# A hybrid diffusion block on one core: another order of steps where the MLP begins

## The chip, the cores and the metric

The kernel runs on one core of one Trainium2 chip. The metric is the device time of one execution in microseconds (us): the median over the runs shown, lower is better. A core has engines that run side by side, each with its own queue of instructions worked off strictly in order: TensorE (PE, with its weight loads as PEld), VectorE (DVE), ScalarE (ACT), GpSimd (POOL) and SyncE (SP). Transfers (DMA) are issued by SP, ACT and POOL; only those of POOL can add to what is already at their destination.

## What is computed

One layer of a diffusion backbone over 1024 tokens of width 1024, with 256 context tokens. What matters here is the seam between its two halves: the output projection of the mixer, the residual with its two row norms, and the first matrix of the MLP.

```python
attn_x = _neighbourhood_attention(q_x, k_x, v_x, k_c, v_c, rpb[l])
mix_x = jnp.concatenate([_pool_mixer(u_x, pool_w[l], pool_scale[l]), attn_x], axis=-1) @ w_out[l]
x = x + gt1 * _rmsnorm(mix_x, g_post_mix[l])
y_x = _sq_relu_mlp(_modulate(x, g_pre_mlp[l], sh2, sc2), w_mlp_in[l], w_mlp_out[l])
x = x + gt2 * _rmsnorm(y_x, g_post_mlp[l])
```

`_modulate` is a row norm times (1 + scale) plus shift, `_sq_relu_mlp` is `square(relu(h @ w1)) @ w2` with `w1` 1024 x 4096.

## The kernel before

**Products.** Every float32 product is made of three matrix products: each operand is split into a high part (a cast on ACT) and a low part (a difference on DVE), and `three` (lines 168 to 170) issues high x high, low x high and high x low as 128x512 matmuls. The large products (output projection, both MLP matrices) use a scheme with seven products of half-size blocks instead of eight. For the first MLP matrix the tokens are cut in two halves (row tiles 0 to 3 and 4 to 7) and the 1024 channels in two halves, which gives the token blocks B11, B21 (first token half, lower and upper channels) and B12, B22 (second token half), and four combinations T1 = B12 - B11, T2 = B22 - T1, T3 = B22 - B12, T4 = B21 - T2. The weights are cut into A11, A12, A21, A22, with combinations S1 to S4 made on the fly by `weight_parts` (line 1207).

**Before the MLP.** The region `added` (line 1043) does most of the output projection for row tiles 0 to 3, then their rows: `out_less` (a difference of sums, DVE), `out_square` (its mean square, ACT), `out_gated` (times the gate, DVE), `row_root` (one over root: a small DVE step and one on POOL), `row_added` (the residual: DVE `xr`, a store on POOL's queue, and its mean square on ACT, `mp<-xr`), `row_second` (the second root) and `row_scaled` (DVE).

**The MLP's beginning.** `last_product` (line 1128) does the last product of the projection, `out_sums(v[t])` for t = 0 to 3, and between these makes channel pairs 0 to 2 of the first token half: eight transposes on PE into `px` (line 1114), a scale and shift on ACT into `nf` (line 1119), and the split into `thB..` (ACT, line 143) and `tlB..` (DVE, line 144), together `pair_made`. In the same list stand the row steps of tiles 4 to 7. `last_pair` (line 1160) makes pair 3 and ends the rows of tiles 4 to 7. ACT and DVE run `last_product` in exactly the order in which it is written (`in_order`, line 103), and so they do with `last_pair` and with the first call of `second_half`.

**The loop.** For p = 0, 2, 4, 6 the kernel does `first_sum` (line 1296) of p and p + 1: twelve matmuls of A11 with B11 into the bank `phx`, then a copy of it on ACT (`s1`, line 1304), stored to memory for p < 4. Then `second_sum` (line 1309) of both adds A12 x B21 to the same bank, for which the copy must have been taken, and squares its positive part on ACT (lines 1246, 1247). Between these `second_half` (line 1172) makes the second token half: 32 transposes, then T2, T1, T3, and after the loop B22 and T4, each as a combination on DVE (lines 1184 to 1189) and a split. PE's order is that in which the program is written, from the region `added` to the last pair; outside the `in_order` parts ACT's and DVE's orders are chosen by a planner. After the loop come sixteen `block_pair`s, each starting with `phy` = S2 x T2.

**Weights.** A generator with a lookahead of four (`lookahead`, line 1269) makes the weights' splits `wpA`, `wpS` ahead of the product that uses them. Four buffers `raw` take the loaded weights, eight `hl` their splits.

Of the kernel before, what the change touches and what calls it, by code (L numbers as in the profile page):

```python
# [1 line left out]

# [8 lines left out]
F32 = mybir.dt.float32  # L11
# [68 lines left out]
def hybrid_block(ctx, tc, x, ctx_in, w_mod, b_mod, gp1, gp2, w_in, pool_w, rpb, w_out, w1, w2, vectors,  # L80
                 mask, edge, out):
    nc = tc.nc
# [59 lines left out]
    def split(src, hi, lo):  # L142
        nc.scalar.copy(hi, src)  # L143
        nc.vector.tensor_tensor(lo, src, hi.bitcast(F32), sub)  # L144

# [835 lines left out]
    with tc.tile_pool(name="ps2", bufs=6, space=PSUM) as ps2:  # L981
# [6 lines left out]
      with ExitStack() as tmp2:  # L988
# [54 lines left out]
        with tc.issue_after(projected[ET.DVE]), tc.issue_after(projected[ET.Activation]), in_order(ET.Activation, ET.DVE) as added:  # L1043
# [47 lines left out]
            for t in (6, 7):  # L1091
                out_square(1, t, c[t])
                out_gated(1, t, c[t])
# [9 lines left out]

        tok = {}
# [3 lines left out]
        def normal_pair(b, kp, both=True):  # L1108
            f = page(f"nf{b}_{kp}")
            for o in range(2):  # L1110
                k = 2 * kp + o
                pt = bank(f"px{b}_{k}")
                for i in range(4):
                    nc.tensor.transpose(pt[:, i * P : (i + 1) * P], mp1[4 * b + i][:, k * P : (k + 1) * P], ident)
                fo = f[:, o * 512 : (o + 1) * 512]
                if b and o and both:
                    nc.vector.tensor_scalar(fo, pt, a2[:, k : k + 1], s2[:, k : k + 1], mul, add)
                else:
                    nc.scalar.activation(fo, pt, AF.Identity, bias=s2[:, k : k + 1], scale=a2[:, k : k + 1])
            return f  # L1120
# [5 lines left out]


        def last_product():
            def pair_made(kp):
                plain[0, kp] = normal_pair(0, kp)  # L1130
                token_part("B11" if kp < 2 else "B21", kp % 2, plain[0, kp])

            def first_steps(t):
                c[t] = out_less(0, t, v[t - 4], u2[t - 4])
                out_square(0, t, c[t])
                out_gated(0, t, c[t])

            def last_steps(t):
                row_second(t)
                row_scaled(t)  # L1140
# [10 lines left out]
            out_sums(v[3], "A22", wt4, 3, False)  # L1151
# [8 lines left out]
        def last_pair():  # L1160
            plain[0, 3] = normal_pair(0, 3)
            token_part("B21", 1, plain[0, 3])
            row_root(7)
            row_added(7)
            for t in (4, 5, 6, 7):
                row_second(t)
                row_scaled(t)

        held = {}


        def second_half(names):
            if not held:
                nf = dict((kp, normal_pair(1, kp, kp % 2 == 0)) for kp in (0, 2, 1, 3))
                nf = [nf[kp] for kp in range(4)]
                held["b12"], held["B22"] = nf[:2], nf[2:]
                held["T1"], held["T2"] = [[page(f"t{i}_{kp}") for kp in range(2)] for i in (1, 2)]
            b12, b22, b21 = held["b12"], held["B22"], [plain[0, 2 + kp] for kp in range(2)]
            for name in names:
                for kp in range(2):  # L1180
                    t1, t2 = held["T1"][kp], held["T2"][kp]
                    src = {"T1": t1, "T2": t2, "T3": b12[kp], "B22": b22[kp], "T4": b21[kp]}[name]
                    if name == "T2":
                        nc.vector.tensor_tensor(t1, b12[kp], plain[0, kp], sub)
                        nc.vector.tensor_tensor(t2, b22[kp], t1, sub)
                    elif name == "T3":
                        nc.vector.tensor_tensor(src, b22[kp], src, sub)
                    elif name == "T4":
                        nc.vector.tensor_tensor(src, src, t2, sub)
                    token_part(name, kp, src)  # L1190

        with tc.issue_after(added[ET.DVE]), tc.issue_after(added[ET.Activation]), in_order(ET.Activation, ET.DVE) as first_part:
            last_product()
# [13 lines left out]
        def weight_parts(p, which):  # L1207
# [13 lines left out]
            for n in which:  # L1221
                if n == "S2":
                    combined("S1", a[1, 0], a[1, 1], add)
                    combined("S2", made["S1"], a[0, 0], sub)
                elif n == "S3":
                    combined("S3", a[0, 0], a[1, 0], sub)
                elif n == "S4":
                    combined("S4", a[0, 1], made["S2"], sub)
# [3 lines left out]
                split(src, blocks(w[:, :512]), blocks(w[:, 512:]))  # L1232
                yield w
# [35 lines left out]
        def lookahead(gens, n):  # L1269
            ahead = []  # L1270
            for g in gens:
                for w in g:
                    ahead.append(w)
                    if len(ahead) > n:
                        yield ahead.pop(0)
            yield from ahead

# [12 lines left out]
        parts = lookahead([early_sequence()], 4)  # L1290

        def step(ps, name, begin):
            product(ps, next(parts), name, begin)
# [40 lines left out]
        def block_pair(p, ahead):  # L1334
# [20 lines left out]
            nc.vector.tensor_tensor(c22, v, c22, add)  # L1355
# [8 lines left out]
            nc.vector.tensor_tensor(c12, z, u2, add)  # L1364
# [80 lines left out]
        for p in range(0, EARLY, 2):  # L1445
            both = [q for q in (p, p + 1) if q < EARLY]
            xs = {}
            for q in both:
                xs[q], early[q] = first_sum(q)
                if q == 0:  # L1450
                    with tc.issue_after(first_part[ET.DVE]), tc.issue_after(first_part[ET.Activation]):
                        with in_order(ET.Activation, ET.DVE):
                            last_pair()
            if p == 2:
                with in_order(ET.Activation, ET.DVE) as made_first:
                    second_half(("T2",))
            if p == 4:
                second_half(("T1",))
            if p == 6:
                second_half(("T3",))  # L1460
            for q in both:
                second_sum(q, xs[q])
        second_half(("B22", "T4"))
        parts = lookahead([sequence()], 4)
        with tc.issue_after(made_first[ET.Activation]), tc.issue_after(made_first[ET.DVE]):
# [151 lines left out]
```

## Time and profile before

| | |
|---|---|
| median of 3 runs | 1064.68 us |
| lowest, highest | 1064.08, 1065.23 us |
| the profiled execution | 1064.99 us |
| its span in the trace | 1063.2 us |
| PE busy | 1036.0 us (97%) |
| DVE, ACT, POOL busy | 713.7 us (67%), 531.4 us (50%), 84.3 us (8%) |
| mean granted clock of PE | 0.992 |

The span runs from the first to the last instruction in the trace; 1.8 us of the profiled execution lie around it. In rows of the timeline the columns are the start in us, the duration in us, the engine, the line, the operation, output <- input by the program's names, shapes and count, and in brackets how long the engine had been idle before it and what ended that. Matmuls overlap, so the pace of PE is read from the distance between two starts. In rows of groups, busy us and the mean in ns stand behind the first bar, idle time before the group and its releasers behind the second.

### The profile page before, as it was taken

The numbers are of one execution on the slowest core, as the hardware profiler recorded it, in microseconds if no ns is written. First come the engines' busy times: TensorE is split into PE (matmuls) and PEld (weight loads), VectorE is DVE, ScalarE is ACT, GpSimd is POOL, SyncE is SP. The second block draws the span as 40 slices with busy tenths as digits, with TensorE's granted clock in tenths as the row PEclk, the third lists the DMA queues.
The fourth block names the chain that finished last, engine by engine and source line by source line (L and its number), as shares of the span: only waits on it lengthen the run. The fifth ranks groups of instructions, "written<-read, shape, count | busy, mean of one in ns | idle before, by whom it ended". The sixth has DMA issues, their size and how long they took to land.

```text
span 1063.2 us, 15505 instructions
## 1 busy us (share of the span) xinstructions
PE 1036.0 (97%) x5878; PEld 851.4 (80%) x5878; DVE 713.7 (67%) x1117; ACT 531.4 (50%) x925; POOL 84.3 (8%) x141
## 2 busy tenths in 40 slices
PE   8999999999999999599999999999999999999996
PEld 6788888877888787488888888888888888888885
DVE  5535646537997598589888766665577566557586
ACT  7462021257887556667555455554463335334441
POOL 2020000051211312100000000000000000000001
PEclk9999999999999999799999999999999999999999
DMA  9905753033337777445766435345597766546556
GB/s 344 322 21 197 278 183 125 21 73 99 71 91 190 170 191 224 138 146 164 255 218 214 152 132 195 126 147 197 204 367 247 248 238 216 192 164 206 174 191 204
DMA packets 104315, 194.87 MB, mean 183 GB/s; under 512 B 7984, under 2 KB 42544, under 8 KB 104240
## 3 DMA queue, kind: packets, MB, share of 16 engines
q1 hardware_dynamic: 81888, 150.82, 43.5%
q10 hardware_dynamic: 16848, 30.44, 7.8%
q0 software_dynamic: 5504, 12.61, 5.5%
q8 instruction: 46, 0.75, 0.3%
q14 instruction: 29, 0.24, 0.1%
HBM read 147.70 MB, written 38.81 MB: 175 GB/s over the span
## 4 chain that ended last, share of the span: by engine, by line
PE 92%; ACT 3%; DMA 2%; DVE 2%; issue 1%; SPq 0%; DVEq 0%; POOLq 0%; ACTq 0%
PE pk L404 4%; PE S L718 3%; PE pa L794 3%; PE phx L169 3%; PE pyv L168 3%; PE pyz L168 3%; PE pyx L169 3%; PE pyx L168 3%; PE phv L170 3%; PE phz L170 3%; PE phv L169 3%; PE phz L169 3%; PE pyv L170 3%; PE pyz L170 3%; PE pyv L169 3%; PE pyz L169 3%
## 5 line engine op out<-in xcount | busy, mean ns | idle before, releaser
L168 PE MATMUL phx<-thB,wpA 128*128 128x512 f32 x128 | 51.9, 406 | 11.8 <-ACT thB L143 9.4
L1246 ACT ACTIVATE c<-c 128x512 f32<-128x512 f32 x48 | 30.4, 633 | 54.9 <-DVE c L1356 23.4
L741 ACT ACTIVATE sp<-sp,nm 128x640 f32<-128x640 f32 (+1 forms) x64 | 51.3, 802 | 8.9 <-DVE nm L732 8.5
L732 DVE CUSTOM_DVE_ANT_0 sp<-S,tab 128x640 f32<-128x640 f32 (+1 forms) x56 | 42.8, 802 | 17.5 <-PE S L718 11.1
L169 PE MATMUL phx<-tlB,wpA 128*128 128x512 f32 x128 | 51.6, 403 | 0.9 <-DVE tlB L144 0.9
L139 POOL TENSOR_TENSOR ry<-vy,nhalf 128x1 f32<-128x1 f32 x8 | 4.4, 550 | 597.5 <-DVE vy L137 597.5
L170 PE MATMUL phx<-thB,wpA 128*128 128x512 f32 x128 | 51.1, 399 | 0.0
L144 DVE TENSOR_TENSOR wpS<-S,wpS 128x512 fp32r<-128x512 f32 x64 | 43.7, 686 | 10.4 <-ACT wpS L143 10.4
L143 ACT CAST wpS<-S 128x512 fp32r<-128x512 f32 x64 | 39.0, 614 | 19.0 <-PE phv L170 10.2
L168 PEld LDWEIGHTS phx<-thB,wpA 128*128 128x128 f32 x128 | 24.9, 194 | 18.4 <-ACT thB L143 10.3
L1247 ACT ACTIVATE c<-c 128x512 f32<-128x512 f32 x48 | 30.3, 632 | 13.2 <-DVE sa L1319 12.4
L169 PEld LDWEIGHTS phx<-tlB,wpA 128*128 128x128 f32 x128 | 24.8, 194 | 7.0 <-DVE tlB L144 1.9
L170 PEld LDWEIGHTS phx<-thB,wpA 128*128 128x128 f32 x128 | 24.9, 194 | 5.1
L718 PE MATMUL S<-kT,q 64*128 64x384 f32 (+1 forms) x128 | 27.9, 495 | 0.4 <-DVE nm L732 0.4
L1364 DVE TENSOR_TENSOR c<-phz,u 128x512 f32<-128x512 f32 x16 | 11.0, 690 | 25.4 <-PE phz L170 25.4
L794 PE MATMUL pa<-pt,v 128*64 128x128 f32 x352 | 25.9, 279 | 0.7 <-ACT px L774 0.2
L779 DVE COPY pt<-T 128x512 f32<-128x512 f32 x32 | 21.9, 686 | 5.4 <-PE T L760 5.4
L168 PE MATMUL phy<-thT,wpS 128*128 128x512 f32 x64 | 24.9, 389 | 0.0
L169 PE MATMUL phy<-tlT,wpS 128*128 128x512 f32 x64 | 24.9, 389 | 0.0
L170 PE MATMUL phy<-thT,wpS 128*128 128x512 f32 x64 | 24.9, 389 | 0.0
L168 PE MATMUL phz<-thT,wpS 128*128 128x512 f32 x64 | 24.9, 389 | 0.0
L169 PE MATMUL phz<-tlT,wpS 128*128 128x512 f32 x64 | 24.9, 389 | 0.0
(1004 smaller groups left out, 3336.6 us busy)
## 6 DMA issues: line engine op xcount, KB each, us to landing
b<-in_w SPq DMA_DIRECT2D x64, 512.0 KB, 4.4
hrS<-hdS SPq DMA_DIRECT2D x32, 512.0 KB, 5.3
hrA<-hdA SPq DMA_DIRECT2D x24, 512.0 KB, 5.7
wm<-in_w_mod SPq DMA_DIRECT2D x16, 512.0 KB, 9.7
wa_0w<-in_w SPq DMA_DIRECT2D x16, 512.0 KB, 4.8
wa_1w<-in_w SPq DMA_DIRECT2D x16, 512.0 KB, 4.3
hdA<-c ACTq DMA_DIRECT2D x32, 256.0 KB, 2.1
hdS<-sa ACTq DMA_DIRECT2D x32, 256.0 KB, 2.7
```

The costliest lines, as they stand in the source:

```text
L143: nc.scalar.copy(hi, src)
L144: nc.vector.tensor_tensor(lo, src, hi.bitcast(F32), sub)
L168: nc.tensor.matmul(ps, ahi, bhi, start=first, stop=False, skip_group_check=more)
L169: nc.tensor.matmul(ps, ahi, blo, start=False, stop=False, skip_group_check=more)
L170: nc.tensor.matmul(ps, alo, bhi, start=False, stop=last, skip_group_check=more)
L404: nc.tensor.matmul(pks[b][j], wk(wgt, k, low, j * P, P), r, start=(k == 0 and n == 0), stop=(k == KT - 1 and n == 2))
L718: nc.tensor.matmul(S[e][:, c0 : c0 + keys.shape[1]], q[hs, cols], keys[hs], start=True, stop=True)
L732: nc.vector.tensor_tensor_reduce(out=to, in0=s, in1=bt, scale=1.0, scalar=BIG, op0=add, op1=ALU.min, accum_out=nm)
L741: nc.scalar.activation(sp, sp, AF.Exp, bias=least[i, e], scale=-1.0, accum_out=sums[i][:, e : e + 1])
L794: nc.tensor.matmul(pa[e * HD : (e + 1) * HD, cols], v[:, f : f + HD], turns[i][:, e, c] if c < 4 else fifths[i][:, :, (e + 1) * HD : (e + ...
L1246: nc.scalar.activation(r, src, AF.Relu)
L1247: nc.scalar.activation(r, r, AF.Square)
```

## The change

Four edits in the MLP's beginning, and one in how weights are made ahead.

1. **Order in `last_product`.** The rows of tiles 4 to 7 leave it, but for `out_less`; the steps of c[6] and c[7] for the other half of the columns come in from `added`. All four channel pairs of the first token half are made here, the last two with their 16 transposes in a row, ahead of the first `first_sum`.
2. **Rows in steps.** `row_steps` is a generator whose six steps are taken one after each of the first sums and second sums (none after `first_sum(3)`).
3. **Second half in steps.** `second_steps` follows with seven: the transposes and `nf` of the second half, the combinations, and one step each for the splits of T2, T1, T3, B22 and T4.
4. **Signs and adding transfers.** B21 and B12 are made with the opposite sign (`less_a2`, `less_s2`), so that every combination becomes a sum: T1' = B11 - B12 and T2 stay on DVE, T3 = B22 - B12 and T4' = T2 - B21 are made by `add_to`, a transfer on POOL's queue that adds to its destination, four of 512 KB in all. A12, A22 and S4 change sign to match (`less_split`), and two results are subtracted where they were added. In `block_pair`s and in the loop nothing else changes.
5. **Weights one by one.** `more` makes one weight part per `step`, with five made in `last_product`. The whole stretch, from `last_product` to the last `second_sum`, stands in one `in_order` for ACT and DVE, transfers that ACT issues among them.

```diff
+    def less_split(src, hi, lo):
+        nc.scalar.activation(hi, src, AF.Copy, scale=-1.0)
+        nc.vector.scalar_tensor_tensor(lo, src, -1.0, hi.bitcast(F32), mul, sub)
...
-            for t in (6, 7):
-                out_square(1, t, c[t])
-                out_gated(1, t, c[t])
...
+        def normal_pair(b, kp, pts, both=True):
+            f = page(f"nf{b}_{kp}")
+            a, d = (less_a2, less_s2) if b == (kp < 2) else (a2, s2)
...
         def last_product():
             for t in range(2):
                 out_sums(v[t], "A22", wt4, t, False)
-            first_steps(4)
-            pair_made(0)
+            first_less(4)
+            more()
+            pts = transposed(0, 0)
+            first_less(5)
+            pair_made(0, pts)
+            more()
             out_sums(v[2], "A22", wt4, 2, False)
-            row_root(4)
-            first_steps(5)
-            row_added(4)
-            pair_made(1)
+            pts = transposed(0, 1)
+            first_less(6)
+            gate_steps(1, 6)
+            pair_made(1, pts)
+            more()
             out_sums(v[3], "A22", wt4, 3, False)
-            row_root(5)
-            first_steps(6)
-            row_added(5)
-            pair_made(2)
-            row_root(6)
-            first_steps(7)
-            row_added(6)
+            pts = transposed(0, 2)
+            first_less(7)
+            pair_made(2, pts)
+            pts = transposed(0, 3)
+            more()
+            pair_made(3, pts)
+            gate_steps(1, 7)
...
+        def row_steps():
+            gate_steps(0, 4)
+            yield
+            row_root(4)
+            gate_steps(0, 5)
+            row_root(5)
+            row_added(4)
+            gate_steps(0, 6)
+            yield
+            row_second(4)
+            row_root(6)
+            row_added(5)
+            gate_steps(0, 7)
+            yield
+            row_second(5)
+            row_root(7)
+            row_added(6)
+            row_scaled(4)
+            yield
+            row_second(6)
+            row_added(7)
+            row_scaled(5)
+            yield
+            row_second(7)
+            row_scaled(6)
+            row_scaled(7)
+            yield
+
+        def second_steps():
+            nf = dict((kp, normal_pair(1, kp, transposed(1, kp), kp % 2 == 0)) for kp in (0, 2, 1, 3))
+            b12, b22, b21 = [nf[0], nf[1]], [nf[2], nf[3]], [plain[0, 2 + kp] for kp in range(2)]
+            yield
+            t1, t2 = [[page(f"t{i}_{kp}") for kp in range(2)] for i in (1, 2)]
+            for kp in range(2):
+                nc.vector.tensor_tensor(t1[kp], b12[kp], plain[0, kp], add)
+                add_to(b12[kp], b22[kp])
+                nc.vector.tensor_tensor(t2[kp], b22[kp], t1[kp], add)
+                add_to(b21[kp], t2[kp])
+            yield
+            for name, src in (("T2", t2), ("T1", t1), ("T3", b12), ("B22", b22), ("T4", b21)):
                 for kp in range(2):
+                    token_part(name, kp, src[kp])
+                yield
...
         def step(ps, name, begin):
-            product(ps, next(parts), name, begin)
+            more()
+            product(ps, ready.pop(0), name, begin)
             flush()
...
+        with tc.issue_after(added[ET.DVE]), tc.issue_after(added[ET.Activation]), in_order(ET.Activation, ET.DVE) as first_part:
+            last_product()
+            between = chain(row_steps(), second_steps())
+            for p in range(0, EARLY, 2):
+                both = [q for q in (p, p + 1) if q < EARLY]
+                xs = {}
+                for q in both:
+                    xs[q], early[q] = first_sum(q)
+                    if q != 3:
+                        next(between)
+                for q in both:
+                    second_sum(q, xs[q])
+                    next(between, None)
+        with tc.issue_after(first_part[ET.Activation]), tc.issue_after(first_part[ET.DVE]):
             reload(0)
             block_pair(0, lambda: None)
```

`add_to` is the helper that the output projection uses already, at line 876 of the profile: `nc.gpsimd.dma_start(to, more, accum_op=add)`.

More of the change, by code (lines that the diff above doesn't have):

```diff
@@ L1 @@
 from contextlib import ExitStack, contextmanager
+from itertools import chain, islice
 import numpy as np
@@ L1090, in hybrid_block, with transposed @@
             c[7] = out_less(1, 7, s5[3], v[3])
-            for t in (6, 7):
-                out_square(1, t, c[t])
-                out_gated(1, t, c[t])
             for t in range(4, 8):
                 row_load(t)
+        less_a2, less_s2 = sm("na2", 8), sm("ns2", 8)
+        nc.vector.tensor_scalar_mul(less_a2, a2, -1.0)
+        nc.vector.tensor_scalar_mul(less_s2, s2, -1.0)
         tok = {}
         plain = {}
-        def normal_pair(b, kp, both=True):
-            f = page(f"nf{b}_{kp}")
+        def transposed(b, kp):
+            pts = []
             for o in range(2):
@@ L1125, in token_part, with pair_made @@
             tok[name, kp] = hi, lo
-        def last_product():
[L1129 to L1140, printed above, removed]
+        def pair_made(kp, pts):
+            plain[0, kp] = normal_pair(0, kp, pts)
+            token_part("B11" if kp < 2 else "B21", kp % 2, plain[0, kp])
@@ L1172, in second_half @@
[L1172 to L1179, printed above, removed]
-                for kp in range(2):
[L1181 to L1190, printed above, removed]
@@ L1231, in weight_parts @@
                 w = whl.tile([P, 1024], F32R, tag="hl", name=f"wp{n}_{p}")
-                split(src, blocks(w[:, :512]), blocks(w[:, 512:]))
+                (less_split if n in ("A12", "A22") else split)(src, blocks(w[:, :512]), blocks(w[:, 512:]))
                 yield w
@@ L1267, in keep @@
             nc.scalar.dma_start(kept(name, p), src)
[L1269 to L1276, printed above, removed]
         def early_sequence():
@@ L1288, in sequence, with more @@
                                         ("A11", "S2", "S1", "S3", "A12", "S4", "A22"))
-        parts = lookahead([early_sequence()], 4)
+        coming_parts, ready = chain(early_sequence(), sequence()), []
+        def more():
+            ready.extend(islice(coming_parts, 1))
         def step(ps, name, begin):
-            product(ps, next(parts), name, begin)
+            more()
+            product(ps, ready.pop(0), name, begin)
             flush()
@@ L1363, in block_pair @@
             c12 = part(f"c12_{p}")
[L1364 removed]
+            nc.vector.tensor_tensor(c12, u2, z, sub)
             squared(c12, c12)
@@ L1444, in hybrid_block @@
         two_sums = page("s1")
[L1445 to L1465, printed above, removed]
+        with tc.issue_after(added[ET.DVE]), tc.issue_after(added[ET.Activation]), in_order(ET.Activation, ET.DVE) as first_part:
[12 more added lines that the diff above has]
+        with tc.issue_after(first_part[ET.Activation]), tc.issue_after(first_part[ET.DVE]):
             reload(0)
```

30 lines of the change are left out of this document (15 added, 15 removed).

## The prediction

> **What bounds the kernel now.** I read the busy shares first, then PE's groups with the idle time before them (370 to 460 us), then the stretches around the MLP's beginning.
>
> ```profile
> PE 1036.0 (97%) x5878; PEld 851.4 (80%) x5878; DVE 713.7 (67%) x1117; ACT 531.4 (50%) x925; POOL 84.3 (8%) x141
> ```
> ```profile
> L168 PE MATMUL phx<-thB,wpA 128*128 128x512 f32 x24 | 11.4, 475 | 11.8 <-ACT thB L143 9.4 <-DVE co L998 1.2 <-ACT s L1304 1.2
> ```
> ```profile
> 414.00:455.00 41.00, 28.26 (x116) 21.53 (x116) 26.90 (x43) 25.10 (x44) 6.65 (x12) 0.83 0.59 181
> 455.00:490.00 35.00, 35.00 (x173) 29.52 (x172) 31.05 (x36) 26.76 (x41) 0.77 (x1) 1.00 0.42 134
> 490.00:600.00 110.00, 110.00 (x487) 91.13 (x486) 93.92 (x148) 59.10 (x101) 0.00 (x0) 1.00 0.64 211
> ```
> PE sets the end: it is busy 97% of the span. Between 414 and 455 it is busy 28.26 of 41 us (first number behind the length; the clock is the third from the end, 0.83), and from 455 on it never waits. The change touches nothing that PE does after `phy`, and PE's instructions up to `phy` are the same, so its price is the shift of `phy`'s start. PE's timeline shows where the time goes:
>
> ```profile
> 414.50 1.03 PE L1114 MATMUL px<-ident,mp 128*128 128x128 f32 x8
> ...
> 429.89 0.80 PE L168 MATMUL phx<-thB,wpA 128*128 128x512 f32 x1 [4.27 <-ACT thB L143]
> ...
> 445.75 0.79 PE L168 MATMUL phx<-thB,wpA 128*128 128x512 f32 x1 [5.13 <-ACT thB L143]
> ...
> 449.30 0.63 PE L168 MATMUL phx<-thB,wpA 128*128 128x512 f32 x1
> 451.01 0.63 PE L169 MATMUL phx<-tlB,wpA 128*128 128x512 f32 x1
> ...
> 455.63 0.39 PE L170 MATMUL phx<-thB,wpA 128*128 128x512 f32 x1
> 458.35 0.39 PE L170 MATMUL phx<-thB,wpA 128*128 128x512 f32 x1
> 458.58 3.65 PE L1114 MATMUL px<-ident,mp 128*128 128x128 f32 x32
> 461.99 0.48 PE L168 MATMUL phx<-thB,wpA 128*128 128x512 f32 x1
> 489.29 0.39 PE L168 MATMUL phy<-thT,wpS 128*128 128x512 f32 x1
> ```
> ```profile
> PE phx L169 <- DVE tlB L144: 0.9, 2, 0.5
> ```
> Idle: 11.8 before the group's first kind of matmul, 9.4 of it the two waits of 4.27 and 5.13, and 0.9 before the second kind: 12.7 us. Full pace is 0.227 us (twelve matmuls from 455.63 to 458.35), slow pace 0.43 (four from 449.30 to 451.01), a transpose 0.107 (32 from 458.58 to 461.99). From 414.50 to 489.29 PE has 216 matmuls and 64 transposes, 49.0 + 6.8 us; of the 74.8 us some 6.3 remain for the slow pace after the two long waits, about 3 each. So the ceiling of the gain is 12.7 + 6.3 = 19 us, with `phy` at 470.3.
>
> **The first waits go.** With the rows of tiles 4 to 7 gone from ACT and DVE's list, `thB` no longer stands behind `mp<-xr`, which took the waits of 4.27 and 5.13. All 32 transposes of the first half, 48 matmuls (two sums, two first sums) run through: 414.50 + 3.4 + 10.9 = 428.8. That cover holds: `px` 3 ends at 418.9, two `nf` of 0.72, a cast of 1.04 and a low part of 1.22 (rows below) end at 422.6, and PE comes to them at 424.8.
>
> **The rows return as a first new wait.** Now the copy `s1` of `phx` 2 stands on ACT, in the written order, behind the rows. Durations:
>
> ```profile
> 410.72 0.62 ACT L130 ACTIVATE jo<-co 128x512 f32<-128x512 f32 x1
> ...
> 421.82 0.61 ACT L143 CAST wpA<-wa3w 128x512 fp32r<-128x512 f32 x1
> 422.34 0.61 ACT L143 CAST wpA<-wa2w 128x512 fp32r<-128x512 f32 x1
> ...
> 438.32 1.07 ACT L1304 COPY s<-phx 128x512 f32<-128x512 f32 x2
> ...
> 442.13 1.06 ACT L130 ACTIVATE mp<-xr 128x1024 f32<-128x1024 f32 x1 [1.67 <-DVE xr L1029]
> 443.19 1.43 ACT L1119 ACTIVATE nf<-px,s,a 128x512 f32<-128x512 f32 x2
> 444.65 1.04 ACT L143 CAST thB<-nf 128x1024 fp32r<-128x1024 f32 x1
> ...
> 479.24 0.63 ACT L1247 ACTIVATE r<-r 128x512 f32<-128x512 f32 x1
> 479.90 0.33 ACTq L1267 DMA_DIRECT2D hdA<-r  x1
> ```
> ```profile
> 426.16 0.68 DVE L144 TENSOR_TENSOR wpA<-wa2w,wpA 128x512 fp32r<-128x512 f32 x1
> 426.76 0.68 DVE L144 TENSOR_TENSOR wpA<-wa3w,wpA 128x512 fp32r<-128x512 f32 x1
> ...
> 440.82 1.28 DVE L1029 SCALAR_TENSOR_TENSOR xr<-mp,rm,xr 128x1024 f32<-128x1024 f32 x1
> 445.73 1.22 DVE L144 TENSOR_TENSOR tlB<-nf,thB 128x1024 fp32r<-128x1024 f32 x1 [3.63 <-ACT thB L143]
> 446.87 0.15 DVE L137 SCALAR_TENSOR_TENSOR vm<-ssm,ssm 128x1 f32<-128x1 f32 x1
> ```
> Back to back a cast takes 0.52 (421.82 to 422.34), a low part 0.60 or, 1024 wide, 1.14 (445.73 to 446.87). From `px` 4 at 422.3, ACT does two pairs of `nf` (1.43 each), two `thB` (0.97), `jo` 0.62, two casts, then the copy of `phx` 0 (0.59): with small waits, 429.6; PE waits 0.8. Then store 0.34, `jo`, cast, copy of `phx` 1, store, `jo`: 432.75; `xr` 4 on DVE to 434.1; `mp` 1.06, `jo` 0.62, cast 0.61: 436.5. Now a turn between the two engines, once a row: low part 0.63, two `vm` 0.12, `xr` 1.28, `mp` 1.06, `jo` 0.62, cast 0.61, two handovers 0.1 = 4.4 us. The turn of row 5 ends at 440.9; row 6 adds 0.63 + 0.12 + 1.28 + 1.06 + 0.1 and then cast 0.52, copy 0.59: 445.2. PE, 48 matmuls after 429.6, came there at 440.5: a **wait of 4.7 us** for ACT's copy.
>
> **The second half brings a second one.** PE goes on at the slow pace for 5.3 us, which is 12 of 24 matmuls: the two second sums end at 453.3, with the last one's drain 453.4. Behind them on ACT: the square of `phx` 3 with its store, 0.63 + 0.66 + 0.34, six `nf` 4.3, a cast: 460.05. DVE, which waited for that cast in the written order, then has no gap: low part 0.6, the four sums of T1' and T2, low part, two low parts of T2 (2.28), low part: 469.0. The last sum ends at 465.5; from there ACT does T2's second cast 0.97, a weight's 0.52, the square of `phx` 4 with its store 1.63, T1's casts 1.93, a weight's, the square of `phx` 5: 472.7.
>
> ```profile
> 461.25 1.22 DVE L1184 TENSOR_TENSOR t<-nf,nf 128x1024 f32<-128x1024 f32 x1
> 462.57 1.23 DVE L1185 TENSOR_TENSOR t<-nf,t 128x1024 f32<-128x1024 f32 x1
> 477.46 0.68 DVE L1219 TENSOR_TENSOR S<-wa_0w,wa_1w 128x512 f32<-128x512 f32 x1
> ```
> (1.22 each for the sums.) Then T3: casts on ACT at 472.7 and 473.7, low parts on DVE to 476.1, S1 and S2 for the next weight 0.7 each, its cast 0.52, and only then the copy of `phx` 6: 478.65. PE, through 32 transposes and 72 matmuls from 453.3, arrives at 473.05: a **wait of 5.6 us**. Queued on ACT behind T3's casts, and so late with them, are that cast, the copies of `phx` 6 and 7 and B22's casts; S1's and S3's parts are due 7 and 5 us before PE uses them, so nothing else comes late. Behind the wait 24 matmuls, 5.4, and one slow period, 2.7 (between 2.5, for 5.3 us at 0.43 in place of 0.227, from 445.75 to 451.01, and 3.1, half of the 6.3): `phy` at 486.8. Handovers that I rounded: 0.2.
>
> **The adding transfers.** T3's casts wait for two of four; the sums before them end at 461.9, 463.1, 464.3, 465.5, and so the transfers are issued. The nearest rows:
>
> ```profile
> 226.00:229.00 3.00, 3.00 (x15) 2.48 (x14) 1.28 (x2) 2.06 (x4) 3.00 (x8) 1.00 0.50 87
> ```
> ```profile
> 357.26 0.86 POOL L876 DMA_DIRECT2D to_2w<-to_0w  x1 [2.79 <-DMA to_2w<-in_w_out]
> 359.12 0.86 POOL L876 DMA_DIRECT2D to_3w<-to_1w  x1 [1.00 <-DMA to_3w<-in_w_out]
> ```
> ```profile
> y<-y POOLq DMA_DIRECT2D x1, 256.0 KB, 3.3
> ```
> ```profile
> to_2w<-to_0w POOLq DMA_DIRECT2D x1, 512.0 KB, 8.6
> to_3w<-to_1w POOLq DMA_DIRECT2D x1, 512.0 KB, 10.8
> ```
> Alone, 256 KB landed in 3.3 us, 1.5 of it transfer (share 0.50 of 3 us). So I estimate 3.0 for 512 KB: the third, T3's second page, lands at 461.9 + 1.8 + 9.0 = 472.7, or up to 475 with the loads and stores then under way; it is needed at 473.7. Under load two landed at 365.9 and 369.9, 4.0 apart: the third of four then at 461.9 + 8.6 + 8.0 = 478.5. POOL's own queue holds them up by nothing: its last root for the rows ends 10 us before. SP's loads go out when a weight's low part frees a buffer, 20 us ahead of their use. Bounds 0 and 4.8 us on the path; the transfers' share from 455 to 490 is 0.42 (the second figure from the end), so the unloaded row is nearer, and I take 0.4. The sums that leave DVE (four of 1.22) gain nothing: PE waits there for the order on ACT. The signs (`less_split`) cost at most 1.28 against 1.22 per 1024, on DVE, 94 of 110 us busy in the block pairs: nothing on the path; without that slack 0.06 us a block.
>
> **Sum.** `phy` at 486.8 + 0.2 + 0.4 = 487.4 against 489.29: -1.9 us. The profiled execution, 1064.99, would be 1063.1; the median of the runs, 0.3 lower, 1062.8.
>
> The Trainium skill, "TensorE: Matmul & The Clock Gate", Part 1, has the array at half rate after an idle window of about 3.4 us and back after as much work. By it a slow period costs an estimated 1.6 us, not 2.7, and the time would be 1061.7; here the pace was still slow 5.3 us after the return at 445.75, so the row decides.
>
> **Rivals.**
> - *The adding transfers land late; slower.* DVE works through from 460 to 478, and POOL's transfers queue behind one another. Place: the cast of T3's second page. Price: one us per us beyond 473.7, the change loses from 476.0 on; at the loaded spacing, 478.5, `phy` starts at 491.8, 1067.2. For: a plain store of POOL's queue landed in 10.1 once; against: the row doesn't say what ran beside it, and it is no adding transfer.
>
> ```profile
> x<-xr POOLq DMA_DIRECT2D x1, 512.0 KB, 10.1
> ```
> The Trainium skill, "SBUF — State Buffer", SBUF: two separate sides, says that some forms of DVE work lock GpSimd out of a port that it needs to write transfers' descriptors; no run here shows it so far.
> - *The clock stays up; faster.* If the second wait doesn't bring the slow pace, 2.7 us less: 1060.1. For: the two waits of 1.2 in the row of the group are followed by no slow row that I found; against: 4.27 was enough, and both new waits are longer.
> - *Nothing is won.* The order moves the waits and their sum stays: 1064.7. For: 0.8 + 4.7 + 5.6 = 11.1 is near to 12.7; against: the turn's rows are measured ones.
>
> **How the numbers follow.** Forecast 0.62, late transfers 0.18, clock 0.14, nothing 0.06. A change under 0.2% (2.1 us) is what a measurement of this kernel can hardly tell from none. The forecast's own range, 1061.2 to 1064.9 (slow period 2.5 to 3.1, transfers 0 to 2, and a us either way for small waits in the two chains, not all at their ends together), lies on both sides of -0.2%: 0.30 faster, 0.31 within, 0.01 slower. Faster 0.30 + 0.14 = 0.44; slower 0.01 + 0.17 = 0.18; within 0.38. Range 1060.0 to 1067.2: both rivals' times.
>
> **What would show it.** PE's waits for `thB` gone; one of 4 to 5 us for `s1` before the second sum of `phx` 2, one of 5 to 6 before that of `phx` 6, each followed by matmuls 0.43 apart; ACT's cast of T3 waiting little or nothing for a transfer; no wait of PE after `phy`. I am wrong if PE waits where I have none, if a wait for `s1` is missing, or if T3's cast waits over 2 us.

## The result, and the profile after

| | before | after |
|---|---|---|
| median of the runs | 1064.71 us (9) | 1061.36 us (9) |
| lowest, highest | 1064.08, 1066.15 | 1060.75, 1063.29 |
| the profiled execution, its span | 1064.99, 1063.2 | 1062.89, 1061.1 |
| ratio, 95% interval | | 0.9971 [0.9961, 0.9981] |

The change gains 3.35 us by the medians, where 1.9 was forecast; the time is 1.4 us below the predicted 1062.8 and inside its range. The two profiled executions differ by 2.1 us, all of it ahead of `phy`. The profile's page on the changed kernel has the same groups at the top; the waits for `thB` are gone from that of `phx`:

```profile
PE 1037.5 (98%) x5878; PEld 853.6 (80%) x5878; DVE 709.6 (67%) x1115; ACT 531.9 (50%) x925; POOL 91.5 (9%) x145
L173 PE MATMUL phx<-thB,wpA 128*128 128x512 f32 x128 | 52.8, 413 | 10.5 <-ACT s L1329 10.5
```

The three stretches (start and end, length, then the busy time of PE, PEld, DVE, ACT and POOL with their instructions; at the end PE's granted clock, the transfers' share and GB/s):

```profile
414.00:455.00 41.00, 36.12 (x171) 29.64 (x170) 28.68 (x45) 30.89 (x55) 11.23 (x12) 0.92 0.62 206
455.00:490.00 35.00, 29.40 (x127) 24.07 (x126) 25.77 (x30) 24.97 (x36) 3.47 (x4) 0.90 0.64 163
490.00:600.00 110.00, 110.00 (x487) 91.10 (x486) 94.62 (x151) 58.90 (x101) 0.00 (x0) 1.00 0.65 216
```

Between 414 and 455 PE is busy 36.1 us instead of 28.3; but from 455 to 490, where it never waited, it now lacks 5.6 us and its clock is 0.90. PE's timeline of the changed kernel has the three waits:

```profile
429.36 0.50 PE L173 MATMUL phx<-thB,wpA 128*128 128x512 f32 x1 [0.39 <-ACT s L1329]
...
445.03 0.80 PE L173 MATMUL phx<-thB,wpA 128*128 128x512 f32 x1 [4.50 <-ACT s L1329]
...
450.74 0.40 PE L174 MATMUL phx<-tlB,wpA 128*128 128x512 f32 x1
...
453.28 3.65 PE L1120 MATMUL px<-ident,mp 128*128 128x128 f32 x32
478.87 0.79 PE L173 MATMUL phx<-thB,wpA 128*128 128x512 f32 x1 [5.60 <-ACT s L1329]
...
487.23 0.39 PE L173 MATMUL phy<-thT,wpS 128*128 128x512 f32 x1
```

`phy` starts at 487.23 (before: 489.29), and what follows it is as long as before: 1061.1 - 487.23 = 573.9, before 1063.2 - 489.29 = 573.9. ACT's timeline of the changed kernel shows what each wait stood behind, first the rows (`mp<-xr`), then T3 (`thT<-nf`):

```profile
438.47 1.06 ACT L131 ACTIVATE mp<-xr 128x1024 f32<-128x1024 f32 x1 [0.94 <-DVE xr L1034]
...
442.84 1.06 ACT L131 ACTIVATE mp<-xr 128x1024 f32<-128x1024 f32 x1 [0.94 <-DVE xr L1034]
...
444.40 0.58 ACT L1329 COPY s<-phx 128x512 f32<-128x512 f32 x1
...
472.91 1.99 ACT L144 CAST thT<-nf 128x1024 fp32r<-128x1024 f32 x2 [0.73 <-ACT r L1277]
477.71 0.62 ACT L144 CAST wpS<-S 128x512 fp32r<-128x512 f32 x1 [2.81 <-DVE S L1249]
478.24 0.58 ACT L1329 COPY s<-phx 128x512 f32<-128x512 f32 x1
```

Two rows are 4.37 us apart (438.47 to 442.84), the turn of 4.4 us, and the copy of `phx` 2 comes behind the third. The casts of T3 wait for no transfer (both had landed by then; the rows stand further down, under the adding transfers); the copy of `phx` 6 waits, by way of a weight's cast, for S1 and S2 on DVE, which stand behind T3's low parts.

### The profile page after: what moved, and what is told of

Same layout as the page of the kernel before. It is cut to its first block, busy times and chain, and to the rows that moved or that the text cites. A ratio compares the mean times of both kernels' runs of the same rounds, so it can differ in the third digit from the quotient of the medians.

```text
span 1061.1 us, 15511 instructions
## 1 busy us (share of the span) xinstructions
PE 1037.5 (98%) x5878; PEld 853.6 (80%) x5878; DVE 709.6 (67%) x1115; ACT 531.9 (50%) x925; POOL 91.5 (9%) x145
## 4 chain that ended last, share of the span: by engine, by line
PE 92%; ACT 4%; DVE 2%; issue 1%; DMA 1%; SPq 0%; ACTq 0%; POOL 0%; DVEq 0%; POOLq 0%
PE pk L409 4%; PE S L723 3%; PE pa L799 3%; PE pyv L174 3%; PE pyv L173 3%; PE pyz L174 3%; PE pyz L173 3%; PE pyx L174 3%; PE phv L175 3%; PE phz L175 3%; PE pyx L175 3%; PE phz L173 3%; PE phv L173 3%; PE phv L174 3%; PE phz L174 3%; PE pyx L173 3%
## 5 line engine op out<-in xcount | busy, mean ns | idle before, releaser
L1389 DVE TENSOR_TENSOR c<-u,phz 128x512 f32<-128x512 f32 x16 | 11.0, 686 | 25.0 <-PE phz L175 25.0
```

## The experiments

Times below stand beside the kernel before on the same chip. "After" in a comparison is the changed kernel on the chip of the first four experiments.

**The changed kernel once more**, unedited.

> The changed kernel itself, once more. Theory: its runs lie 2.5 us apart because the two slow periods of the clock (13 and 14 slow steps from matmul to matmul, 5.7 us more than full pace together in the first profile) are not equally long in each execution: the time should again lie between 1060.7 and 1063.3 us, and in this profile what is between the last instruction's end and the start of phy should be 573.9 us, as in the first, within 0.3, while the time up to phy and the number of slow matmuls differ. Rival: the executions differ elsewhere; then phy starts at 487.2 within 0.3 with 27 slow steps again, and the stretch behind it is what differs.

1062.51 us (1061.13 to 1062.68, 6 runs) against 1064.92, 0.9968 [0.9955, 0.998]. Waits 0.39, 4.48 and 5.61; the stretch behind `phy` 573.9; from the first transpose to `phy` 72.4 us instead of 72.9, and 24 slow steps instead of 27 (a slow step is a start of a matmul about 0.43 us behind the one before it, instead of 0.227). What differs lies in the slow periods and ahead of the first transpose (0.3 us). This execution's time is near that of the first profile, so by itself it shows little of the 2.5 us; the granted clock shows more. The stretches of half a microsecond in the first profile in which its two slow periods begin and end (the clock is the third figure from the end):

```profile
443.50:444.00 0.50, 0.00 (x0) 0.00 (x0) 0.00 (x0) 0.50 (x3) 0.50 (x3) 0.92 0.41 50
450.50:451.00 0.50, 0.50 (x4) 0.37 (x3) 0.50 (x1) 0.45 (x1) 0.38 (x1) 0.75 0.06 25
478.00:478.50 0.50, 0.00 (x0) 0.00 (x0) 0.14 (x1) 0.50 (x2) 0.00 (x0) 0.55 1.09 377
484.50:485.00 0.50, 0.50 (x3) 0.37 (x2) 0.50 (x2) 0.00 (x0) 0.00 (x0) 0.62 0.00 0
```

A mean of 0.92 over half a microsecond that falls from 1.0 to 0.5 puts the edge at 443.92; the others are at 450.75, 478.05 and 484.88. They lie 6.83, 27.30 and 6.83 apart: 2, 8 and 2 times 3.41 us. So in this execution the clock falls and rises at ticks 3.41 us apart, and each half-rate stretch lasts two of them, the first part of it inside the wait. Where the ticks fall against the wait differs from execution to execution: here the first fall came 1.1 us ahead of the return from the wait (445.03), and by the same working 1.9 us ahead in the second execution (443.46 for 445.32). The granted clock of the nine runs above agrees: the five with spans of 1059.0 to 1059.6 us have a mean of 0.993 or 0.994, the four of 1060.2 to 1061.5 have 0.992, and 0.001 of the span is about a us.

**T3 and T4' as sums on DVE.**

```diff
-                add_to(b12[kp], b22[kp])
+                nc.vector.tensor_tensor(b12[kp], b12[kp], b22[kp], add)
...
-                add_to(b21[kp], t2[kp])
+                nc.vector.tensor_tensor(b21[kp], b21[kp], t2[kp], add)
```

> T3 and T4' as sums on DVE at the same places, in place of the four adding transfers. Theory: ACT's and DVE's written order is one chain up to the copy of phx 6, so four sums of 1.22 us more on DVE, less the gaps DVE has in that stretch (1.44 us before T3's low parts), come out at the end of it: the wait before the second sum of phx 6 grows from 5.6 to 9.0 us, phy starts at 490.7 instead of 487.2, and the time is 1064.9 us (1064.0 to 1065.5). Rival, as the prediction had it: sums that leave DVE gain nothing; then the wait stays 5.6 and the time 1061.4 within 0.7.

1066.15 us, 1.001 [1.0001, 1.0019]: 3.6 us more than after, a little more than before, and above the expected 1064.0 to 1065.5. PE's timeline of this kernel:

```profile
482.55 0.80 PE L173 MATMUL phx<-thB,wpA 128*128 128x512 f32 x1 [9.01 <-ACT s L1329]
```

`phy` at 490.68, as expected. The sums do count: the written order makes DVE a part of the chain to that copy. Without the transfers the change gains nothing (1.001, with them 0.9968).

**The transfers alone, in the kernel before.**

```diff
-                        nc.vector.tensor_tensor(src, b22[kp], src, sub)
+                        add_to(src, b22[kp])
...
-                        nc.vector.tensor_tensor(src, src, t2, sub)
+                        add_to(src, t2)
```

> The kernel before, with T3 and T4 made by adding transfers at the same places and nothing else changed (the signs are not, so this kernel computes B12 + B22 and B21 + T2). Theory: before, PE waits for nothing from 455 on, so sums that leave DVE gain nothing, and the transfers cost nothing: 1064.7 us (1063.9 to 1065.5), phy at 489.3. Rival: the adding transfers are what the change gains by; then about 3.5 us less, 1061.2. Second rival: they land late for T3's casts, which the planner put right behind them; then a wait of some us before phv of the first block pair, 1067 or more.

1065.53 against 1065.62, 1.000 [0.9991, 1.0009], no gain, as expected; `phy` 74.84 us behind the first transpose, before 74.79. The same transfers that carry 3.6 us in the new order are worth nothing in the old one, where PE did not wait behind 455.

**Every transfer twice**, one more `add_to` of the same pages behind each.

> Each of the four adding transfers is issued twice (T3 becomes B12 + 2 B22 and so on, so the output is another one). Theory: the transfers' queue serves one after the other, 3.0 us each (47.3% of 25 us for four in the changed kernel's profile), so T3's second page, fourth of four pairs in the queue's order at sixth place, lands at 463 + 18 + 1 = 482 instead of 471; the cast of T3's second page, at 473.9 in the changed kernel, then waits some 8 us for a transfer, and phy moves by as much: 495 (492 to 498), 1070 us (1067 to 1074). So late adding transfers cost one us per us. Rival: transfers overlap, or T3 has more slack than 2 to 3 us; then phy moves by less than 3 us.

1069.86 us, 1.0044 [1.0028, 1.006]. ACT's timeline of this kernel:

```profile
474.84 1.04 ACT L144 CAST thT<-nf 128x1024 fp32r<-128x1024 f32 x1 [4.01 <-DMA nf<-nf]
481.75 1.04 ACT L144 CAST thT<-nf 128x1024 fp32r<-128x1024 f32 x1 [5.86 <-DMA nf<-nf]
485.41 0.62 ACT L144 CAST wpS<-S 128x512 fp32r<-128x512 f32 x1 [2.62 <-DVE S L1251]
485.93 0.58 ACT L1331 COPY s<-phx 128x512 f32<-128x512 f32 x1
```

The cast of T3's second page starts at 481.75, forecast 482, though the planner issued the transfers in another order than I assumed. The copy of `phx` 6 is 7.7 us later than in the changed kernel. `phy` is only 6.4 later (493.58), since the slow period behind this wait was 7 steps, not 14 (1.55 us of slow pace instead of 2.90). Late transfers cost one us per us, as the rival had it.

**The splits of T3, B22 and T4 one place later.**

```diff
                     second_sum(q, xs[q])
-                    next(between, None)
+                    if q != 5:
+                        next(between, None)
```

> No step behind the second sum of phx 5, so the splits of T3, B22 and T4 move one place back each, and the copy of phx 6 comes ahead of T3's casts. Theory: the wait of 5.6 us is the written order alone; it falls to 2.2 us (the copy then waits for the low parts of T1 and for S1 and S2 on DVE), too short to bring the slow pace, and phy starts at 481.4: 5.8 us less, 1055.6 us (1054.8 to 1057.0). Rival: nothing is won, since T3 or B22 or T4 are then late in the first block pair by what was gained; the time stays above 1060 and PE waits after phy. Half-way case: a wait of 2.2 still brings a slow period of 2.8, 1058.4.

1059.69 us, 0.9947 [0.9932, 0.9962]. PE's timeline, then ACT's:

```profile
473.89 0.50 PE L173 MATMUL phx<-thB,wpA 128*128 128x512 f32 x1 [1.82 <-ACT s L1329]
...
490.84 0.50 PE L173 MATMUL phz<-thB,wpS 128*128 128x512 f32 x1 [2.85 <-ACT c L1376]
```
```profile
482.89 2.01 ACT L144 CAST thT<-nf 128x1024 fp32r<-128x1024 f32 x2 [0.40 <-ACT r L1277]
486.98 0.62 ACT L144 CAST wpS<-S 128x512 fp32r<-128x512 f32 x1 [2.08 <-DVE S L1249]
...
490.21 0.58 ACT L1376 COPY c<-phz 128x512 f32<-128x512 f32 x1
```

The wait of 5.6 falls to 1.82 and `phy` starts at 479.67, earlier than expected. But 577.8 us follow it instead of 573.9: T4's casts and low parts now stand ahead of the copy of `phz`, in the first block pair. Both theories are half right, and the time missed the range of the first: half of the gain was given back. The wait of 1.82 brought no slow step.

**The rows taken apart:** `row_added` cut in two, its sum on DVE (`row_sum`) and its mean square on ACT (`row_square`), the second taken one step later.

```diff
             row_root(4)
             gate_steps(0, 5)
             row_root(5)
-            row_added(4)
+            row_sum(4)
             gate_steps(0, 6)
             yield
-            row_second(4)
+            row_square(4)
             row_root(6)
-            row_added(5)
+            row_sum(5)
             gate_steps(0, 7)
+            row_second(4)
             yield
...
```

> The mean square of each row on ACT is taken one step later than its sum on DVE, so that the weight's cast does not stand behind it. Theory: the wait of 4.5 us for the copy of phx 2 is the turn between ACT and DVE, 4.4 us a row; with the turn opened the wait falls to 1.0, its slow period goes, a wait of 2.2 for the last scaled row comes before the second half's transposes, the wait for the copy of phx 6 is 4.8, and phy starts at 482.2: 5.0 us less, 1056.4 us (1055.4 to 1058.5). Rival: the rows themselves are the bound and the whole wait moves to the transposes; the time stays at 1060 or more, with a wait of 4 us or more for mp there.

1057.12 us, 0.9921 [0.9907, 0.9936]; `phy` at 482.29. PE's timeline:

```profile
441.94 0.50 PE L173 MATMUL phx<-thB,wpA 128*128 128x512 f32 x1 [0.72 <-ACT s L1339]
449.96 5.05 PE L1126 MATMUL px<-ident,mp 128*128 128x128 f32 x29 [1.94 <-DVE mp L1049]
...
475.16 0.80 PE L173 MATMUL phx<-thB,wpA 128*128 128x512 f32 x1 [3.81 <-ACT s L1339]
```

The wait of 4.5 was the turn. Of it 1.9 comes back at the transposes, where the last scaled row is now what PE waits for, and the clock fell to one half among them (5.05 us for 29 transposes; two of the kernels below took 3.39); the rival's 4 us did not come.

**Both.**

> The rows taken apart and the splits of T3, B22, T4 one place later, in one kernel. Theory: the two waits and what follows them are independent, so phy starts at 475.9 (no wait of PE over 2.3 us ahead of it); but ACT's list up to the last square of phx 7 ends at 485.5 and the copy of phz 0 (c22) behind it at 487.2, while PE comes to the product of B22 at 484.1, so that a wait of 3 us, seen already with the splits alone (2.85), stays behind phy. Time 475.9 + 573.9 + 3.4 + 1.8 around the span = 1055.0 us (1053.5 to 1056.5). Rival: the two gains are one and the same; then the time is that of the rows taken apart alone, 1057.1, or more.

1056.54 us, 0.9912 [0.9896, 0.9927], just above the expected range; `phy` at 476.24, as forecast. The wait behind it is there, and so, what I had not counted, is a slow period of 14 steps behind it (2.9 us):

```profile
487.43 0.79 PE L173 MATMUL phz<-thB,wpS 128*128 128x512 f32 x1 [2.87 <-ACT c L1386]
```

In time this can't be told from the rows alone.

**Both, with T4's split in the first block pair.**

```diff
-                    if q != 5:
+                    if q not in (5, 6, 7):
                         next(between, None)
...
-            block_pair(0, lambda: None)
+            block_pair(0, lambda: next(between, None))
```

> As the kernel before it, with the split of T4 moved out of the written order into the first block pair. Theory: the wait for the copy of phz 0 was T4's split (1.93 us on ACT, 2.28 on DVE) standing ahead of it; without it the copy comes at 483 and PE does not wait behind phy: 475.9 + 573.9 + 1.8 = 1051.6 us (1050.5 to 1053.0). Rival: T4's split is then late itself, PE comes to T4 at 486.8; a wait for it in the first block pair, and no gain on the kernel before it.

1054.34 us, 0.9891 [0.9876, 0.9905]: below both kernels, but 2.7 us above the forecast and outside its range. PE's timeline, and a stretch of the same kernel:

```profile
441.51 0.50 PE L173 MATMUL phx<-thB,wpA 128*128 128x512 f32 x1 [0.73 <-ACT s L1339]
449.52 3.39 PE L1126 MATMUL px<-ident,mp 128*128 128x128 f32 x29 [1.92 <-DVE mp L1049]
470.17 0.50 PE L173 MATMUL phx<-thB,wpA 128*128 128x512 f32 x1 [0.93 <-ACT s L1339]
...
498.56 0.50 PE L173 MATMUL phz<-thB,wpS 128*128 128x512 f32 x1 [0.53 <-ACT c L1386]
...
502.56 0.50 PE L173 MATMUL phv<-thT,wpA 128*128 128x512 f32 x1 [0.94 <-DVE c L1390]
```
```profile
476.00:600.00 124.00, 122.49 (x537) 100.22 (x536) 106.11 (x169) 67.16 (x114) 0.00 (x0) 1.00 0.63 210
```

`phy` starts at 475.92, as forecast, and the wait for the copy of `phz` 0 is gone. The 2.6 us are lost behind it. From `phy` on PE issues the same matmuls in the same order as in the changed kernel; laid start by start beside it, it falls back by 0.17 us at 488.78, by 0.83 at the wait of 0.53, by 1.28 at that of 0.94 and by 0.32 at 513.77. So a stop of PE costs some 0.3 us beyond the idle time in its row: the last matmul before it takes its full 0.39, where the next would have started after 0.227, and the first step behind it takes 0.34. The clock is at 1.00 throughout (last row). Why ACT and DVE are late at these places is not shown.

**This kernel once more**, unedited.

> The fastest kernel so far once more, in more rounds: 0.989 of the kernel before, 1054 us (1053.2 to 1055.3) if its time is as steady as it should be without slow periods of the clock (its runs should lie closer together than the changed kernel's 2.5 us). Rival: it varies as much, so the variation was not the slow periods'.

1054.38 us (1053.59 to 1054.80, 4 runs), 0.9893 [0.9879, 0.9908]; `phy` at 477.39. Its runs lie 1.2 us apart, the four before 1.8, the changed kernel's nine 2.5. That leaves the question open, for this kernel isn't free of slow periods: in this execution the transposes ran slow, in the one above they did not (3.39). PE's timeline:

```profile
449.79 5.05 PE L1126 MATMUL px<-ident,mp 128*128 128x128 f32 x29 [1.92 <-DVE mp L1049]
```

**The planner in the loop:** `in_order` ends with `last_product`.

> The written order ends with last_product; in the loop of first and second sums ACT's and DVE's order is chosen by the planner, with the same steps and the same transfers. In its list the casts and mean squares of the rows lie closer to the sums on DVE (two mean squares of c ahead of the first row's), and S1's and S2's sums for the first block pair come ahead of T3's low parts, while T3's casts still stand ahead of the copy of phx 6. Theory: the waits are the written order's, so the first falls as in the kernel with the rows apart (0.7 to 1.5 us) and the second to 2 to 4 us; phy at 477 to 483, 1055.5 us (1053 to 1059). Rival: the steps' places in the program set the waits, whoever orders within them; then both stay within a us of 4.5 and 5.6, and the time at 1061 or more.

1055.49 us, 0.9902 [0.9886, 0.9919]. PE's timeline:

```profile
442.21 0.50 PE L173 MATMUL phx<-thB,wpA 128*128 128x512 f32 x1 [0.67 <-ACT s L1329]
...
472.54 0.51 PE L173 MATMUL phx<-thB,wpA 128*128 128x512 f32 x1 [4.76 <-ACT s L1329]
...
492.11 0.50 PE L173 MATMUL phv<-thT,wpA 128*128 128x512 f32 x1 [1.36 <-DVE c L1380]
```

The time is as expected, the waits only in part: the first goes (0.67), the second stays at 4.76, for the planner too puts T3's casts ahead of the copy of `phx` 6. ACT's timeline:

```profile
470.95 1.05 ACT L144 CAST thT<-nf 128x1024 fp32r<-128x1024 f32 x1 [0.78 <-DMA nf<-nf]
```
Here the second cast waits for its transfer, so up to 0.78 of the 4.76 is the adding transfers': the casts come some 4 us earlier than in the changed kernel, the transfers only some 1.6. The first wait was the order within steps, the second where T3's step is taken.

**Work for PE inside the waits.**

```diff
+                if p in (2, 6):
+                    junk = bank(f"fill{p}")
+                    for i in range(26 if p == 2 else 36):
+                        nc.tensor.transpose(junk[:, (i % 4) * P : (i % 4 + 1) * P], ident, ident)
                 for q in both:
                     second_sum(q, xs[q])
```

> The changed kernel with transposes of a constant, which nobody reads, in front of the second sums of phx 2 (26) and phx 6 (36): work for PE inside its two waits, 2.8 and 3.9 us, leaving 1.7 us of each idle. Theory: the slow pace comes from the idle time, not from the place; with idle stretches of 1.7 us each it does not come, the second sums run at 0.227, and phy starts 4 to 5.7 us earlier, at 481.5 to 483.2: 1058.2 us (1056.5 to 1059.5). Rival: transposes do not keep the clock up, or the slow pace is the second sums' own (their operands); then the matmuls behind both waits are 0.43 apart as before and the time stays 1061.4 to 1062.5.

1059.49 us (1059.22 to 1060.12), 0.9941 [0.9925, 0.9958]; `phy` at 483.34, time and `phy` at the slow end of what was expected. PE's timeline:

```profile
440.80 3.00 PE L1483 MATMUL fill<-ident 128*128 128x128 f32 x26
445.43 0.50 PE L173 MATMUL phx<-thB,wpA 128*128 128x512 f32 x1 [1.63 <-ACT s L1329]
445.76 0.39 PE L174 MATMUL phx<-tlB,wpA 128*128 128x512 f32 x1
445.99 0.40 PE L175 MATMUL phx<-thB,wpA 128*128 128x512 f32 x1
...
472.38 4.09 PE L1483 MATMUL fill<-ident 128*128 128x128 f32 x36
477.59 0.50 PE L173 MATMUL phx<-thB,wpA 128*128 128x512 f32 x1 [1.12 <-ACT s L1329]
```

The copies come as late as before, yet the matmuls behind both waits are 0.23 apart and no slow step is left. Two new waits of 0.65 and 0.35 take a us of it. So the slow pace belongs to the idle time and not to the place. The four runs lie 0.9 us apart, the changed kernel's nine 2.5.

## Why the prediction was right, and where it was wrong

- **The bound.** Right. What follows `phy` is 573.9 us in both kernels; the gain is the shift of `phy`, 2.06 us in the profiles. Nothing contradicts the ceiling: with both waits taken away `phy` came to 475.9, 5.6 short of the 470.3, and the waits left ahead of it (0.39, 0.73, 1.92, 0.93) are 4.0 of that. But its 6.3 us were not all slow pace. Two stretches of the kernel before show where its half rate ended:

```profile
434.00:434.50 0.50, 0.50 (x5) 0.50 (x3) 0.16 (x1) 0.50 (x2) 0.50 (x1) 0.52 0.00 0
451.50:452.00 0.50, 0.50 (x4) 0.40 (x3) 0.46 (x1) 0.26 (x1) 0.50 (x1) 0.95 0.55 221
```
  The edges are 434.48 and 451.55, 4.6 and 5.8 us behind the two returns. Less the idle 0.47 in each, half of that is 4.7 us; the other 1.6 are what six stops cost beyond their idle time, some 0.3 each. So the upper bound of 3.1, "half of the 6.3", held more than a slow period.
- **The first waits go.** Right; 0.39 us was left of them, forecast 0.8.
- **The rows as a first new wait.** 4.50 us for a forecast of 4.7, at 445.03 for 445.2. Its cause, the turn between ACT and DVE, is shown by the rows taken apart and again by the planner's order.
- **The second one.** 5.60 for 5.6, at 478.87 for 478.65. Its cause, T3's step ahead of the copy, is shown by T3 later: 1.82.
- **The slow period.** The mechanism held; the size is the term that was off. I took 2.7 each, between 2.5 and 3.1, as if it were a constant: 2.76 and 2.90 in the first profile, 2.4 and 2.7 in the second, and over all experiments 7 to 14 slow steps, 1.55 to 2.9 us. Even the same wait has no one price: the first one (4.46 to 4.51 us) was followed by 2.8, 2.4, 2.4, 1.7 and 1.6 us of slow pace in five executions (the changed kernel's two, the sums on DVE, T3 later, every transfer twice), whose programs differ only behind it. The median of the runs lies 1.5 lower than the profiled execution, not 0.3 as before. That this is the slow periods, shorter in most executions, fits these five and the runs' clocks; a trace of one of the short executions of the changed kernel was not taken. I rejected the rule of the Trainium skill, "TensorE: Matmul & The Clock Gate", Part 1, and the estimate of 1.6 us from it, for the row. The Trainium skill also says there that the window of about 3.4 us runs freely, so that the number of slow matmuls varies from run to run: the edges at 3.41 us agree, and 1.55 to 1.7 is what was seen where the period lasted about one tick behind the return, 2.4 to 2.9 where it lasted more.
- **The sum.** Profile to profile it fits (1063.1 for 1062.89), in part by luck: the second wait ended 0.2 later than forecast, its slow period was 0.2 longer, and the 0.6 for handovers and transfers were not there.
- **The adding transfers.** Forecast 0.4 on the path, found nothing in the changed kernel: the casts of T3 have no wait for them. My estimate of 3.0 us for 512 KB holds. DMA issues and queues of the changed kernel, 455 to 480:

```profile
q0 software_dynamic: 576, 2.10, 47.3%
...
nf<-nf POOLq DMA_DIRECT2D x2, 512.0 KB, 6.1
nf<-t POOLq DMA_DIRECT2D x2, 512.0 KB, 8.6
```
  47.3% of 25 us for four is 2.96 each. And POOL's timeline has the issue of T3's second page, and the DMA issues between 464.8 and 465.2 have its time from there to landing:

```profile
464.61 0.85 POOL L881 DMA_DIRECT2D nf<-nf  x1 [0.49 <-issue]
```
```profile
nf<-nf POOLq DMA_DIRECT2D x1, 512.0 KB, 7.6
```
  It landed at 472.2 (forecast 472.7), some 1.6 us before its cast, the second of the two that start at 472.91. T3's first page, issued at 462.23, landed 4.6 us later, at 466.9. The rival of late transfers had the right price and the wrong landing; but the slack is small, and the planner's order, with earlier casts, waited 0.78 us. Each was issued in 0.85 to 0.90 us, like the 0.86 of before, although DVE ran sums back to back; the lock on a port that the Trainium skill describes for some forms of DVE work ("SBUF — State Buffer", SBUF: two separate sides) does not show here.
- **The sums that leave DVE gain nothing.** This step was wrong, as the prediction put it. It is true of the order before, where PE waited for nothing there (1.000), and I carried it over to the new one, where they are worth 3.6 us. The sum did not suffer, because I had left these four sums out of DVE's part of the new chain anyway; the reader would have drawn the wrong conclusion on what the gain hangs on.
- **The signs.** Nothing, as forecast: no wait behind `phy`.
- **The rivals.** That the clock stays up did not come true in the changed kernel's profiles; the fill, which keeps it up behind both waits, shows that it is worth about 4 us (483.34 for 487.23). That nothing is won is refuted by the interval.

## What to carry to other kernels

When a step is moved in a hand-written order of two engines, look for the next instruction that frees a bank of PE and count everything that stands ahead of it on both engines: the waits here were late by order, not by lack of time, and three small moves (the rows apart, T3's step, T4's) gained another 8 us (0.997 to 0.989 of the time before). What an operation costs belongs to the order it stands in; the same four sums were worth nothing before and 3.6 us after. If PE must wait some microseconds, cheap work for it inside the wait saves the slow period behind it.

## What the runs showed of the hardware

- The granted clock falls to one half and rises again at ticks 3.41 us apart. In the eleven executions here in which it changed between 400 and 520 us, all edges lie on such a grid within 0.02 us, 3.41, 6.83, 10.24 or 13.66 us of half rate at a time (in the changed kernel 443.92 to 450.75 and 478.05 to 484.88). Where the return from a wait falls between two ticks decides how long the slow pace lasts: 7 to 14 steps, 3.0 to 6.0 us in these runs, without regard to the length of the wait (14 steps behind 2.87 us, 7 behind 14.6).
- What seems to count is how much of a stretch between two ticks PE was idle, not the wait as such. In PE's idle times and the edges of these eleven executions, every fall stood at the end of a stretch in which PE had been idle for 56% or more, and stretches of up to 51% (the kernel before, 437.89 to 441.30: a wait of 1.19 us and the start of the next) brought none. A rise came behind stretches idle for at most 9%, none behind 22% or more. So a fall inside a wait lasted two ticks or more (478.05 to 484.88: 24% of its first stretch was still wait), a fall at the return or behind it one (rows apart, 475.15 to 478.56, return at 475.16). This rule is read off these executions; no run tests it by itself.
- So the wait need not be long. One of 2.85 us, cut in two by a tick (40 and 44%, T3 later), was followed by no slow step; one of 2.87, 62% of one stretch (the kernel with both moves), by 14. Of four executions with a wait of 1.92 to 1.94 us before the transposes, two ran 29 of them in 3.39 us, two in 5.05, and one of each is of the same kernel (rows above): where it was slow, 56 and 57% of one stretch was idle, and the granted clock fell to one half about a microsecond after PE had gone on.
